# Two instead of four plain slices in the last feed-forward's first part, with the work around them in another order

## The chip, the cores and the metric

The kernel runs on one core of a Trainium2 chip. The metric is the device time of one execution in microseconds (us). TensorE (PE) does the matmuls and transposes, VectorE (DVE) and ScalarE (ACT) the elementwise work, SyncE's queue (SP) issues most transfers. Each engine works through its own instructions in a fixed order.

## The reference

One inference step of a decoder with two layers, in float32, for a prompt of 1024 tokens and 8 sample tokens that share all weights. Each layer has a mixer and a feed-forward, each between two RMS norms, with a residual behind. The part that the change is about is the feed-forward of the last layer:

```python
def swiglu(h, w_gu, w_down):
    gate, up = jnp.split(h @ w_gu, 2, axis=-1)
    return (jax.nn.silu(gate) * up) @ w_down

h = h + rmsnorm(mix, g[1])
h = h + rmsnorm(swiglu(rmsnorm(h, g[2]), w_gu[l], w_down[l]), g[3])
```

The model width is 1024, the hidden width of the feed-forward 2816, which is 22 slices of 128.

## The kernel before

**Two groups.** The tokens go through as two groups: group 0 holds 512 prompt tokens, group 1 the other 512 and the 8 sample tokens (520 columns, in two halves of 260). Activations lie transposed: 128 features on the partitions, tokens along the free dimension, eight tiles for the model width. Every float32 operand is split into two parts of a faster matmul type: ACT casts it (`split_to`, L286; `split_w`, L266), DVE subtracts the cast from the original, and three matmuls (high times high, high times low, low times high) stand for one.

**A feed-forward of group 1 in the last layer** is the class `ffn_w`. Its 22 slices come in five parts (`PARTS`: 5, 5, 4, 4, 4 slices); each part computes its slices and then projects them down (L696), added up in `R`. A slice is computed in one of two ways:

- *plain* (`gate_up_q`, L528): gate and up each as 8 blocks by 3 by 2 halves, together 96 matmuls of 260 columns and four weight blocks of 128 x 512;
- *seven products* (`gate_up_w`, L553): a scheme of the Strassen kind over 2 x 2 blocks of weights and tokens. Seven products of 12 matmuls (84), seven weight blocks (four of them sums that were put into DRAM earlier), and a few additions in PSUM and on DVE. Between products ACT puts negated partial results into other PSUM banks (L588, L591), DVE combines at the end (L599 to L605).

The products need sums of the token operands. `sums_w` (L355) makes them in four steps, each with 12 DVE rows of 260 columns (L369 full operand, L377 difference, L288 split) and four ACT casts. In part 0 the first four slices are plain (`plain` = 4), and between them the steps of `sums_w` are issued: one behind the first slice, two behind the second, one behind the third, each kept on DVE behind that slice's product of gate and up.

**What runs beside it.** Group 0's feed-forward of the same layer has just ended. Its closing (`f0.finish(False)`: row-sum matmul L332, Ln and Exp on ACT in L333 and L334, then `residual`, DVE rows L457 and L463), the transposes and stores of its output (`store_y`, L1555 to L1560) and the transposes of group 1's own residual into rows (`token_rows`, L513 to L524, which also frees the four buffers of `apool` that hold it) are woven between the steps of `ffn_w`: 17 of theirs to 7 of its. `weave` sets the order in which instructions are recorded; a scheduler then sets the order on each engine, and buffers are handed out from pools of fixed size (PSUM banks `q`, raw weights `w`, split weights `ws`). `residual` reads its input into buffers of the pool whose tag is `x0`, which `sums_w` uses too. From part 1 on, every other raw weight block lies in half a buffer of `apool` (`raws`).

Of the kernel before, what the change touches and what calls it, by code (L numbers as in the profile page):

```python
# [18 lines left out]
P = 128  # L19
# [5 lines left out]
def tile_decoder(  # L25
# [46 lines left out]
    def nm(s):  # L72
        uid[0] += 1
        return f"{s}_{uid[0]}"
# [159 lines left out]
    def weave(*streams):  # L234
        drain(mixed(*streams))
# [49 lines left out]

    def split_to(dst, src):  # L286
        nc.scalar.copy(dst[0], src)  # L287
        nc.vector.tensor_sub(dst[1], src, dst[0].bitcast(F32))  # L288

    def rev(ap):  # L290
        st, n = ap.ap[-1]
# [53 lines left out]
    def normed(g, R, rstd, gc, out, keep=False):  # L345
        n = NG[g]
        for k in range(ND):
            t = N() if keep else R[k]
            nc.vector.scalar_tensor_tensor(t[:, :n], R[k][:, :n], gc(k), rstd[:, :n], op0=ALU.mult, op1=ALU.mult)
            x = X(g)  # L350
            split_to((x[:, 0, :n], x[:, 1, :n]), t[:, :n])
            out.append(x)
            yield

    def sums_w(xs, ops):  # L355

        n, h = NG[1], PW[1]
        for k in range(4):  # L360
            x0, x1 = xs[k], xs[k + 4]
            y = YT()
            if k % 2 == 0:
                z, u = YT(), YT()
            o = (k % 2) * h

            def full(x, c):
                t = B()
                nc.vector.tensor_add(t[:, :h], x[:, 0, c : c + h].bitcast(F32), x[:, 1, c : c + h].bitcast(F32))  # L369
                return t  # L370

            b11, b12, b21, b22 = full(x0, 0), full(x0, h), full(x1, 0), full(x1, h)
            for d, p, a, b in (
                (b11, u[:, :, o : o + h], b12, b11), (b12, y[:, :, h : 2 * h], b12, b22),
                (b22, y[:, :, :h], b22, b11), (b21, z[:, :, o : o + h], b21, b22),
            ):
                nc.vector.tensor_sub(d[:, :h], a[:, :h], b[:, :h])  # L377
                split_to((p[:, 0, :], p[:, 1, :]), d[:, :h])
            ops.append([
                x0[:, :, :h], x1[:, :, :h], x1[:, :, h:n], z[:, :, o : o + h], u[:, :, o : o + h],  # L380
                y[:, :, :h], y[:, :, h : 2 * h],
            ])
            yield
# [54 lines left out]
            out.append(x)  # L438
            yield

    def residual(g, R, rstd, gc, store, acc=None, first=False):
        n = NG[g]
        w = D // 2 if first else n
        ht = [xpool.tile([P, 2, w], F32, tag=f"x{g}", name=nm("ht")) for _ in range(ND // 2)]
        for j in range(ND // 2):
            if first:
                t0 = g * G + j * P
                nc.sync.dma_start(ht[j].rearrange("p a n -> p (a n)"), x_prompt[0, t0 : t0 + P, :])
            else:
                nc.sync.dma_start(ht[j], hs[g][:, 2 * j : 2 * j + 2, :n])  # L450
        for k in range(ND):
            if first:
                ps = NS()
# [3 lines left out]
            nc.vector.scalar_tensor_tensor(R[k][:, :n], R[k][:, :n], gc(k), rstd[:, :n], op0=ALU.mult, op1=ALU.mult)  # L457
            if first:
                nc.vector.tensor_add(R[k][:, :G], R[k][:, :G], ps)
                if g:  # L460
                    nc.vector.tensor_add(R[k][:, G:n], R[k][:, G:n], xsraw[:, k, :])
            else:
                nc.vector.tensor_add(R[k][:, :n], R[k][:, :n], ht[k // 2][:, k % 2, :])  # L463
# [64 lines left out]
    def gate_up_q(l, f, xt):  # L528

        h, n = PW[1], NG[1]  # L530
        sg = T()
        for j in range(2):
            w = split_w(w_gu[l], 0, ND, j * DFF + f * P)
            pp = [Q(2 * j + a) for a in range(2)]
            for k in range(ND):
                wh, wl = w[k]
                for wi, (wt, xi) in enumerate(((wh, 0), (wh, 1), (wl, 0))):
                    for a in range(2):
                        nc.tensor.matmul(  # L539
                            pp[a][:, :h], wt, xt[k][:, xi, a * h : (a + 1) * h],  # L540
                            start=(k == 0 and wi == 0), stop=(k == ND - 1 and wi == 2),
                        )
            for a in range(2):
                d = sg[:, a * h : (a + 1) * h]
                if j == 0:
                    nc.scalar.activation(d, pp[a][:, :h], AF.Silu)
                else:
                    last = nc.vector.tensor_mul(d, d, pp[a][:, :h])
        mt = M(F32R)
        split_to((mt[:, 0, :n], mt[:, 1, :n]), sg[:, :n])  # L550
        return mt, last

    def gate_up_w(l, f, ops, spl, raws):  # L553

# [52 lines left out]
        split_to((mt[:, 0, :n], mt[:, 1, :n]), sg[:, :n])  # L607
        return mt

    sums = {}  # L610

    def part_of(f):
        for i, (f0, nf) in enumerate(PARTS):
# [30 lines left out]
    class ffn_w:  # L644


        def __init__(self, l, x, plain):
            self.g, self.l, self.x, self.ops, self.plain, self.n, self.r, self.pi = 1, l, x, [], plain, 0, 0, 0
            self.R = self.acc = None
            self.half = []  # L650
            self.sums = sums_w(x, self.ops)

        def spl(self):
            self.n += 1
# [13 lines left out]
        def part(self, pi):  # L668
# [4 lines left out]
            for j in range(nf):  # L673
                self.pi = pi
                if f0 + j < self.plain:
                    mt, ins = gate_up_q(l, f0 + j, self.x)
                    mids.append(mt)
                    with tc.issue_after(ins.ins):
                        for _ in range((1, 2, 1, 0)[j]):
                            next(self.sums, None)  # L680
                else:
                    mids.append(gate_up_w(l, f0 + j, self.ops, self.spl, self.raws))
                yield
# [33 lines left out]
    class ffn:  # L717
# [37 lines left out]
        def finish(self, store):  # L755
            rstd = rstd_from(self.acc, NG[self.g], 1.0 / D)
            acc = small([P, WID], tag="st", bufs=3) if store else None
            yield from residual(self.g, self.R, rstd, lambda k: gcol(self.l, 3, k), store, acc)
            if store:
                self.r = rstd_from(acc, NG[self.g], 1.0 / D)  # L760
                yield
# [863 lines left out]
    weave((o1.finish(), 17), (f0.part(4), 8))  # L1625
    banks.close()
    single.append(ctx.enter_context(tc.tile_pool(name="quads", bufs=2, space=PSUM)))
    f1 = ffn_w(1, o1.x, 4)
    weave((chain(f0.finish(False), store_y(0, f0.R), token_rows(1, o1.R)), 17), (chain(f1.part(0), f1.part(1)), 7))
    drain(f1.part(2), f1.part(3), f1.part(4), f1.finish_rows())  # L1630


# [30 lines left out]
```

## Time and profile before

| | us |
|---|---|
| median of 3 runs | 2450.96 |
| lowest and highest run | 2450.86, 2453.5 |
| the profiled execution | 2454.44 |
| its span, first to last instruction | 2452.7 |
| PE busy | 2413.9 |
| DVE busy | 1563.8 |
| ACT busy | 1204.3 |

The profiled execution is one more run of its own, and times in the trace count from the start of its span. A row of a timeline has start, duration, engine, line, operation, output and inputs by the program's names, and in brackets how long the engine stood idle before it and what ended that. Durations of neighbours overlap, so what an instruction costs its queue is the step from one start to the next. In the trace part 0 of the last feed-forward runs from 2070 to 2164 us.

### The profile page before, as it was taken

The page shows a single profiled execution, that of the slowest core. Times are in us where ns is not written, and L with a number is a line of the kernel's source. Part 1 is how long each engine was busy: PE and PEld are TensorE (multiplying, and loading weights), DVE is VectorE, ACT ScalarE, POOL GpSimd, SP SyncE. Part 2 cuts the span into 40 slices and gives each one's busy share as a digit, 9 for nine tenths or more (in the row PEclk, how much of TensorE's full clock was granted, in tenths as well). Part 3 has the DMA queues.
Part 4 walks back from the last instruction along what each step waited for, and adds up shares of the span by engine and source line. Part 5 has one row for each costly group of instructions (what it writes and reads, how often), then busy time and mean ns, then how long its engine had stood idle before and what let it go on. Part 6 is the DMA issues. An engine that isn't in the chain of part 4 may idle for free.

```text
span 2452.7 us, 40619 instructions
## 1 busy us (share of the span) xinstructions
PE 2413.9 (98%) x15473; PEld 2141.9 (87%) x15473; DVE 1563.8 (64%) x2697; ACT 1204.3 (49%) x2354; POOL 102.6 (4%) x153
## 2 busy tenths in 40 slices
PE   7999999999999999999999999999999999999998
PEld 5888988888877887999999989877787898999997
DVE  5777556765775676555544585677677558655665
ACT  4547544444444454555433454555454445564444
POOL 2000000000000000011111100022000000000000
PEclk9999999999999999999999999999999999999998
DMA  5353252263543446686688866453453244375541
GB/s 177 106 157 104 74 159 84 65 178 118 179 136 95 138 146 210 171 221 150 181 201 220 237 187 189 153 163 118 140 154 117 82 126 125 117 200 148 151 134 66
DMA packets 496726, 360.33 MB, mean 147 GB/s; under 512 B 19181, under 2 KB 443738, under 8 KB 496530
## 3 DMA queue, kind: packets, MB, share of 16 engines
q1 hardware_dynamic: 477970, 303.19, 41.2%
q0 software_dynamic: 18560, 54.53, 9.1%
q8 instruction: 122, 2.00, 0.3%
q14 instruction: 74, 0.61, 0.1%
HBM read 327.83 MB, written 75.96 MB: 165 GB/s over the span
## 4 chain that ended last, share of the span: by engine, by line
PE 90%; DVE 4%; DMA 2%; ACT 2%; issue 1%; SPq 0%; POOL 0%; DVEq 0%; ACTq 0%; POOLq 0%
PE mm L280 62%; PE q L581 7%; PE q L696 5%; PE q L539 2%; PE mm L1082 2%; PE s L932 1%; PE s L891 1%; PE s L1265 1%; PE mm L868 1%; PE s L1440 1%; PE mm L841 1%; DMA b<-qd 1%; PE s L1479 1%; PE s L918 1%; DVE ws L267 1%
## 5 line engine op out<-in xcount | busy, mean ns | idle before, releaser
L280 PE MATMUL mm<-x,ws 128*128 128x260 f32 (+1 forms) x7776 | 1330.4, 330 | 0.0
L280 PEld LDWEIGHTS mm<-x,ws 128*128 128x128 f32 x7776 | 1149.2, 188 | 142.9 <-issue 8.2
L266 ACT CAST ws<-w 128x512 fp32r<-128x512 f32 x712 | 420.1, 591 | 685.7 <-PE mm L280 563.6
L267 DVE TENSOR_TENSOR ws<-w,ws 128x512 fp32r<-128x512 f32 x712 | 462.1, 652 | 263.3 <-ACT ws L266 255.7
L280 PE MATMUL mm<-m,ws 128*128 128x512 f32 (+1 forms) x2112 | 393.1, 343 | 0.4 <-DVE r L476 0.4
L280 PEld LDWEIGHTS mm<-m,ws 128*128 128x128 f32 x2112 | 324.3, 189 | 47.3 <-issue 3.4
L696 PE MATMUL q<-m,ws 128*128 128x260 f32 x1056 | 128.8, 283 | 0.0
L696 PEld LDWEIGHTS q<-m,ws 128*128 128x128 f32 x1056 | 127.2, 188 | 0.4 <-ACT hT L514 0.2
L572 DVE TENSOR_TENSOR ws<-w,ws 128x512 fp32r<-128x512 f32 x126 | 86.5, 691 | 59.7 <-ACT ws L571 57.0
L581 PE MATMUL q<-y,ws 128*128 128x260 f32 x864 | 112.9, 283 | 0.0
L571 ACT CAST ws<-w 128x512 fp32r<-128x512 f32 x126 | 78.0, 621 | 67.9 <-PE q L696 27.4
L581 PEld LDWEIGHTS q<-y,ws 128*128 128x128 f32 x864 | 107.6, 188 | 0.0
L476 DVE TENSOR_TENSOR r<-r,mm 128x512 f32<-128x512 f32 (+1 forms) x96 | 66.0, 687 | 59.9 <-PE mm L280 58.8
L320 DVE TENSOR_SCALAR t<-mm 128x512 f32<-128x512 f32 (+1 forms) x74 | 51.2, 692 | 64.3 <-PE mm L280 64.3
L732 DVE TENSOR_TENSOR t<-t,mm 128x512 f32<-128x512 f32 (+1 forms) x66 | 45.5, 689 | 67.9 <-PE mm L280 67.4
L324 DVE TENSOR_TENSOR t<-t,t 128x512 f32<-128x512 f32 (+1 forms) x66 | 45.8, 694 | 65.7 <-ACT t L323 65.7
L581 PE MATMUL q<-x,ws 128*128 128x260 f32 x648 | 86.3, 282 | 0.0
L581 PEld LDWEIGHTS q<-x,ws 128*128 128x128 f32 x648 | 81.3, 188 | 0.0
L343 DVE TENSOR_TENSOR st<-st,n 128x512 f32<-128x512 f32 (+1 forms) x98 | 67.1, 691 | 6.5 <-ACT n L342 5.0
L287 ACT CAST m<-t 128x512 fp32r<-128x512 f32 (+1 forms) x88 | 54.9, 624 | 25.3 <-DVE t L732 16.5
L1018 POOL DMA_INDIRECT c<-in_cache_sb_k,pidx x16 | 16.4, 1026 | 1128.7 <-issue 919.7
L288 DVE TENSOR_TENSOR m<-t,m 128x512 fp32r<-128x512 f32 (+1 forms) x88 | 60.9, 692 | 2.6 <-ACT m L287 1.4
(356 smaller groups left out, 2513.0 us busy)
## 6 DMA issues: line engine op xcount, KB each, us to landing
w<-in_w_gu SPq DMA_DIRECT2D x334, 256.0 KB, 3.1
w<-in_w_down SPq DMA_DIRECT2D x160, 256.0 KB, 2.7
w<-in_w_in_a SPq DMA_DIRECT2D x80, 256.0 KB, 2.9
wsum<-in_w_gu POOLq DMA_DIRECT2D x18, 1024.0 KB, 8.9
w<-wsum SPq DMA_DIRECT2D x72, 256.0 KB, 3.5
w<-in_w_o SPq DMA_DIRECT2D x64, 256.0 KB, 2.7
wsum<-in_w_gu POOLq DMA_DIRECT2D x12, 1280.0 KB, 10.5
w<-in_w_mem_kv SPq DMA_DIRECT2D x32, 256.0 KB, 3.2
```

Source lines behind the costliest of these rows:

```text
L266: nc.scalar.copy(ws[:, 0, :n, :], raw[:, :n, :])
L267: nc.vector.tensor_sub(ws[:, 1, :n, :], raw[:, :n, :], ws[:, 0, :n, :].bitcast(F32))
L280: nc.tensor.matmul(ps[:, a, : PW[g]], wt, xt[k][:, xi, o : o + PW[g]], start=(k == 0 and wi == 0), stop=(k == nk - 1 and wi == 2),)
L287: nc.scalar.copy(dst[0], src)
L288: nc.vector.tensor_sub(dst[1], src, dst[0].bitcast(F32))
L320: nc.vector.tensor_scalar(sv(x, g), pv(ps, g), -44.0, None, op0=ALU.max)
L343: nc.vector.tensor_add(acc[:, :n], acc[:, :n], t[:, :n])
L476: nc.vector.tensor_add(dst, dst, pv(ps, g))
L571: nc.scalar.copy(w[:, 0, :], src)
L572: nc.vector.tensor_sub(w[:, 1, :], src, w[:, 0, :].bitcast(F32))
L581: nc.tensor.matmul(ps[:, :h], w[:, wj, k * P : (k + 1) * P], x[:, xi, :], start=(first and k == 0 and wi == 0), stop=(k == 3 and wi == 2), ...
L696: nc.tensor.matmul(pp[a][:, :h], wt, mids[k][:, xi, a * h : (a + 1) * h], start=(k == 0 and wi == 0), stop=(k == nf - 1 and wi == 2),)
```

## The change

It does four things in the last part. Two slices instead of four are plain, so that 192 matmuls become 168. All four steps of `sums_w` are issued behind the last split of the norm ahead of them (`done`), two after each plain slice, instead of behind the slices' own products. The closing residual of group 0 reads its input into the pool `cpool` (`spare`). And the weave is taken apart: two plain slices alone, then the closing residual and the store of group 0 between the three product slices, then the token rows between the steps of part 0's down projection, then part 1.

```diff
     def split_to(dst, src):
         nc.scalar.copy(dst[0], src)
-        nc.vector.tensor_sub(dst[1], src, dst[0].bitcast(F32))
+        return nc.vector.tensor_sub(dst[1], src, dst[0].bitcast(F32))
...
-            split_to((x[:, 0, :n], x[:, 1, :n]), t[:, :n])
+            ins = split_to((x[:, 0, :n], x[:, 1, :n]), t[:, :n])
             out.append(x)
+            if k == ND - 1:
+                done.append(ins)
...
-        ht = [xpool.tile([P, 2, w], F32, tag=f"x{g}", name=nm("ht")) for _ in range(ND // 2)]
+        ht = [C() if spare else xpool.tile([P, 2, w], F32, tag=f"x{g}", name=nm("ht")) for _ in range(ND // 2)]
...
             self.sums = sums_w(x, self.ops)
+            self.after = done[-1]
...
                 if f0 + j < self.plain:
-                    mt, ins = gate_up_q(l, f0 + j, self.x)
-                    mids.append(mt)
-                    with tc.issue_after(ins.ins):
-                        for _ in range((1, 2, 1, 0)[j]):
-                            next(self.sums, None)
+                    mids.append(gate_up_q(l, f0 + j, self.x))
+                    with tc.issue_after(self.after.ins):
+                        next(self.sums, None)
+                        next(self.sums, None)
...
-    f1 = ffn_w(1, o1.x, 4)
-    weave((chain(f0.finish(False), store_y(0, f0.R), token_rows(1, o1.R)), 17), (chain(f1.part(0), f1.part(1)), 7))
+    f1 = ffn_w(1, o1.x, 2)
+    first = f1.part(0)
+    drain(islice(first, 2))
+    weave((chain(f0.finish(False), store_y(0, f0.R)), 12), (islice(first, 3), 3))
+    weave((token_rows(1, o1.R), 5), (first, 4))
+    drain(f1.part(1))
     drain(f1.part(2), f1.part(3), f1.part(4), f1.finish_rows())
```

Where this moves instructions is shown at three places. Lines stand two further down in the changed kernel from here on (L457 is L459, L546 is L548, L571 is L573). DVE, right behind the last split of the norm (`x`), before; `r` is group 0's sum, `ht` its residual input, `ws` split weights:

```order
L288 TENSOR_TENSOR x_20237<-n_20235,x_20237 128x520
L288 TENSOR_TENSOR x_20242<-n_20240,x_20242 128x520
L457 SCALAR_TENSOR_TENSOR r_16324<-r_16324,par,st_20030 128x512 x2
L463 TENSOR_TENSOR r_16324<-r_16324,ht_20255 128x512 x2
L457 SCALAR_TENSOR_TENSOR r_16324<-r_16324,par,st_20030 128x512
L267 TENSOR_TENSOR ws_20428<-w_20426,ws_20428 128x512
```

After the change the same two rows are followed by 56 others (all the sums and the two plain slices' own rows); these are the last two of them and what stands behind:

```order
L288 TENSOR_TENSOR y_20574<-b_20581,y_20574 128x260
L288 TENSOR_TENSOR y_20552<-b_20579,y_20552 128x260
L574 TENSOR_TENSOR ws_20615<-w_20613,ws_20615 128x512
L574 TENSOR_TENSOR ws_20633<-w_20631,ws_20633 128x512
L574 TENSOR_TENSOR ws_20650<-w_20648,ws_20650 128x512
L574 TENSOR_TENSOR ws_20668<-w_20666,ws_20668 128x512
L288 TENSOR_TENSOR m_20548<-t_20423,m_20548 128x520
L459 SCALAR_TENSOR_TENSOR r_16324<-r_16324,par,st_20030 128x512
L574 TENSOR_TENSOR ws_20687<-w_20685,ws_20687 128x512
L465 TENSOR_TENSOR r_16324<-r_16324,c_20599 128x512
```

The sums (`y`) now stand ahead of the first weight split of a product slice (L574) and the closing residual behind it, between that slice's splits.

ACT, around the closing's Ln (L333) and Exp (L334), before:

```order
L333 ACTIVATE st_20030<-q_20251,epsb 128x512
L287 CAST x_20242<-n_20240 128x520
L334 ACTIVATE st_20030<-st_20030 128x512
L266 CAST ws_20428<-w_20426 128x512
L546 ACT_TABLE_LOAD
L546 ACTIVATE t_20265<-q_20276 128x260
```

And after the change, where L590 is the product slice's first negation and L596 its Silu:

```order
L333 ACT_TABLE_LOAD
L333 ACTIVATE st_20030<-q_20595,epsb 128x512
L287 CAST m_20548<-t_20423 128x520
L334 ACT_TABLE_LOAD
L334 ACTIVATE st_20030<-st_20030 128x512
L590 ACTIVATE q_20610<-q_20609 128x260
L573 CAST ws_20708<-w_20706 128x512
L573 CAST ws_20726<-w_20724 128x512
L593 ACTIVATE q_20611<-q_20610 128x260
L573 CAST ws_20761<-w_20759 128x512
L596 ACT_TABLE_LOAD
L596 ACTIVATE t_20683<-q_20609 128x260
```

Ln and Exp have moved from ahead of the first plain slice's Silu (L546) into the first product slice, and three more table loads stand there.

PE, at the end of the token rows (the sample rows, `8x128`, out of the `apool` buffers `a`), before, where part 0's down projection follows:

```order
L523 MATMUL q_21303<-ident,a_19138 8x128 x2
L523 MATMUL q_21303<-ident,a_19139 8x128 x2
L523 MATMUL q_21309<-ident,a_19140 8x128 x2
L523 MATMUL q_21309<-ident,a_19141 8x128 x2
L696 MATMUL q_21325<-m_20390,ws_21317 128x260
```

And after the change, where part 1's first product follows:

```order
L525 MATMUL q_21499<-ident,a_19138 8x128 x2
L525 MATMUL q_21499<-ident,a_19139 8x128 x2
L525 MATMUL q_21505<-ident,a_19140 8x128 x2
L525 MATMUL q_21505<-ident,a_19141 8x128 x2
L583 MATMUL q_21511<-x_20075,ws_21517 128x260 x3
```

The sample rows' transposes have moved from ahead of 120 of the down projection's matmuls to behind all of them. On ACT their two copies (`c`) now stand directly ahead of part 1's first weight casts:

```order
L705 COPY r_21106<-q_21465 128x260
L526 COPY c_21498<-q_21499 8x512
L526 COPY c_21498<-q_21505 8x512
L573 CAST ws_21517<-w_21515 128x512
L573 CAST ws_21535<-w_21533 128x512
L573 CAST ws_21552<-w_21550 128x512
```

Of these blocks `w_21533` is the first that lies in half an `apool` buffer.

More of the change, by code (lines that the diff above doesn't have):

```diff
@@ L439, in start, with residual @@
             yield
-    def residual(g, R, rstd, gc, store, acc=None, first=False):
+    def residual(g, R, rstd, gc, store, acc=None, first=False, spare=False):
         n = NG[g]
         w = D // 2 if first else n
-        ht = [xpool.tile([P, 2, w], F32, tag=f"x{g}", name=nm("ht")) for _ in range(ND // 2)]
+        ht = [C() if spare else xpool.tile([P, 2, w], F32, tag=f"x{g}", name=nm("ht")) for _ in range(ND // 2)]
         for j in range(ND // 2):
@@ L547, in gate_up_q @@
                 else:
-                    last = nc.vector.tensor_mul(d, d, pp[a][:, :h])
+                    nc.vector.tensor_mul(d, d, pp[a][:, :h])
         mt = M(F32R)
         split_to((mt[:, 0, :n], mt[:, 1, :n]), sg[:, :n])
-        return mt, last
+        return mt
     def gate_up_w(l, f, ops, spl, raws):
@@ L608, in gate_up_w @@
         return mt
-    sums = {}
+    sums, done = {}, []
     def part_of(f):
@@ L757, in finish @@
             acc = small([P, WID], tag="st", bufs=3) if store else None
-            yield from residual(self.g, self.R, rstd, lambda k: gcol(self.l, 3, k), store, acc)
+            yield from residual(self.g, self.R, rstd, lambda k: gcol(self.l, 3, k), store, acc, spare=not store)
             if store:
```

## The prediction

> **What bounds the kernel now.** I read the page's busy shares first, then the table of stretches near the change, then the timelines of TensorE (PE), VectorE (DVE), ScalarE (ACT) and the DMA queue SP in the stretch that the change rewrites.
>
> ```profile
> PE 2413.9 (98%) x15473; PEld 2141.9 (87%) x15473; DVE 1563.8 (64%) x2697; ACT 1204.3 (49%) x2354; POOL 102.6 (4%) x153
> ```
>
> ```profile
> core 0: us, PE busy (x) PEld busy (x) DVE busy (x) ACT busy (x) POOL busy (x), PEclk, DMA share, GB/s
> 2050.00:2100.00 50.00, 48.25 (x323) 43.89 (x322) 48.45 (x90) 26.90 (x48) 0.00 (x0) 1.00 0.28 82
> 2100.00:2150.00 50.00, 50.00 (x424) 49.56 (x423) 28.30 (x63) 28.10 (x65) 0.00 (x0) 1.00 0.41 130
> ```
>
> PE is busy through all of it and the clock is granted in full, so a matmul taken out is worth its own time, and every wait that is put before a matmul costs its own time. The other number to see is DVE between 2050 and 2100: 48.45 of 50 us. DVE is as full as PE just where the change hangs more work in front of PE.
>
> ```profile
> 2070.47 2.03 PE L539 MATMUL q<-x,ws 128*128 128x260 f32 x15 [1.75 <-DVE r L476]
> 2072.33 1.02 PE L332 MATMUL q<-st,ones 128*128 128x512 f32 x2
> 2072.79 44.70 PE L539 MATMUL q<-x,ws 128*128 128x260 f32 x369
> 2117.33 1.91 PE L1555 MATMUL q<-ident,r 128*128 128x128 f32 x16
> ...
> 2127.72 1.61 PE L581 MATMUL q<-y,ws 128*128 128x260 f32 x12
> 2129.16 1.91 PE L1555 MATMUL q<-ident,r 128*128 128x128 f32 x16
> ...
> 2148.90 1.04 PE L523 MATMUL q<-ident,a 128*8 128x128 f32 x8
> 2149.82 14.60 PE L696 MATMUL q<-m,ws 128*128 128x260 f32 x120
> 2164.26 1.59 PE L581 MATMUL q<-x,ws 128*128 128x260 f32 x12
> ```
>
> Lines of the changed kernel stand two further down than these, so L581 is L583 there. These rows are the four plain slices (L539), one slice of seven products (L581), the down projection of part 0 (L696) and the start of part 1 (2164.26). No row after the first has a bracket: PE waits for nothing from 2070.47 to 2164.26.
>
> **Term 1, matmuls saved: -3.0 us.** The 369 plain matmuls begin every (2117.33 - 2072.79) / 369 = 0.1207 us, so a plain slice of 96 takes 11.6 us; a product of 12 takes 1.44 us (2127.72 to 2129.16), a slice of seven 10.1. Two slices change kind: 2 x 1.5 = 3.0 us less. Transposes and down projection stay the same in number. A product slice loads, casts and splits seven weight blocks where a plain one has four: six more loads on SP, casts on ACT and splits on DVE. The loads lie beside (DMA is 0.28 to 0.41 busy above), the splits are counted in term 2.
>
> **Term 2, the first product slice waits for DVE: +4.3 us (2.5 to 6).** DVE works in order. What an instruction takes from the next one there is read from these rows:
>
> ```profile
> 2075.25 1.41 DVE L457 SCALAR_TENSOR_TENSOR r<-r,par,st 128x512 f32<-128x512 f32 x2
> 2076.57 1.28 DVE L463 TENSOR_TENSOR r<-r,ht 128x512 f32<-128x512 f32 x2
> ...
> 2085.74 0.42 DVE L369 TENSOR_TENSOR b<-x 128x260 f32<-128x260 f32 x1
> 2086.08 0.42 DVE L377 TENSOR_TENSOR b<-b,b 128x260 f32<-128x260 f32 x1
> 2086.42 0.68 DVE L463 TENSOR_TENSOR r<-r,ht 128x512 f32<-128x512 f32 x1
> 2087.02 0.42 DVE L288 TENSOR_TENSOR y<-b,y 128x260 fp32r<-128x260 f32 x1
> ```
>
> A 260-wide row takes 0.34 us of the queue (2085.74 to 2086.08), a 512-wide one 0.60 (2086.42 to 2087.02), a scale-and-multiply of 512 takes 0.66 (1.32 for two). The last norm row leaves DVE at 2075.25, and nothing ahead of it changes on DVE. Before, the closing residual of the first half stands there. Now the 56 rows up to the first weight split of a product slice are 48 rows of operand sums (16.3), 4 products with up (1.4), one middle split and three weight splits (2.4): 20.1 us, so that split starts at 2095.4 and is ready 0.7 later, at 2096.1. ACT's casts for the sums are as many as before and lie beside.
>
> PE gets there earlier: 2070.47 + 192 x 0.1207 = 2093.6, and 0.46 for the row-sum matmul L332 (2072.33 to 2072.79, moved here) makes 2094.1. Four matmuls need only the cast half of their weights (0.5), then PE waits from 2094.6 to 2096.1: 1.5 us.
>
> Next on DVE, up to the first split of the third and last product slice: 14 weight splits and 2 middle splits (9.6), the closing residual's eight L457-kind rows (5.3) and eight L463-kind rows (4.8), six rows of the slices' combinations (2.0) = 21.7, so that slice's weights are ready at 2117.8. PE wants them after 14 products (20.2) and 8 transposes (1.91 / 16 x 8 = 0.9): at 2115.2. So the wait is 2.5 us in all even if DVE never waits itself. But it does, in two ways. Behind the first product slice's last product, DVE has a combination row (L606 after the change), a residual row and only then the next slice's weight split: 0.2 (a product's last matmul ends that long after the next has begun: 1.61 against 1.44) + 0.34 + 0.66 + 0.68 = 1.9 us, against which PE has four transposes and two matmuls (0.7), so 1.2 more. And the residual's root-mean-square chain is now issued in the middle of the product slice, where it costs ACT table loads:
>
> ```profile
> 2073.39 0.69 ACT L333 ACTIVATE st<-q,epsb 128x512 f32<-128x512 f32 x1
> 2073.98 0.62 ACT L287 CAST x<-n 128x520 fp32r<-128x520 f32 x1
> 2074.50 0.63 ACT L334 ACTIVATE st<-st 128x512 f32<-128x512 f32 x1
> 2075.03 0.61 ACT L266 CAST ws<-w 128x512 fp32r<-128x512 f32 x1
> 2075.65 1.28 ACT L546 ACT_TABLE_LOAD   x1
> ...
> 2120.72 0.37 ACT L588 ACTIVATE q<-q 128x260 f32<-128x260 f32 x1 [0.54 <-PE q L581]
> ```
>
> Before, Ln (L333) and Exp (L334) ran with the table that was there and one load followed, Silu's. Now Silu's load comes first, then Ln, Exp and Silu again each bring one: three loads more, 3.8 us of ACT. Behind Exp's load waits ACT's negation of the first product (L590), which PE's third product adds onto. ACT is through it at 2094.6 + 1.3 (load) + 0.6 (Ln) + 0.5 (a middle cast) + 1.3 (load) + 0.5 (Exp) + 0.4 (the negation, L588 now) = 2099.2; PE's first two products end at 2096.1 + 20 x 0.12 = 2098.5. That is 0.7 more. 2.5 + 1.2 + 0.7 = 4.4; since these waits partly overlap DVE's own lateness, I take 4.3. The lower end is DVE's sum alone, 2.5; the upper end adds two further handovers of 0.8 us each (one for each remaining slice).
>
> The closing residual's input now has buffers of its own and is read long ahead; no wait for it is seen now, so this is worth nothing here. The store's and the rows' transposes now come eight banks in a row, 3.7 us of PE; ACT's and DVE's evictions at some 0.6 each run beside them on two engines, so I cost them at nothing (if one engine had to do all eight alone, 1.1).
>
> **Term 3, part 1 starts late: +3.0 us (2.0 to 4.7).** Now the sample rows' transposes (L523) come at 2148.90, 15.4 us before part 1. After the change they are the last thing ahead of part 1. They free the buffers into which the second weight block of part 1 is loaded:
>
> ```profile
> SPq L566 <- PE q L523: 1.0, 1, 1.0
> ```
> ```profile
> 2149.31 1.08 SPq L566 DMA_DIRECT2D w<-wsum  x2
> ```
> ```profile
> 2150.12 1.05 ACT L524 COPY c<-q 8x512 f32<-8x512 f32 x2
> 2152.84 0.62 ACT L571 CAST ws<-w 128x512 fp32r<-128x512 f32 x1 [1.67 <-DMA w<-wsum]
> ...
> 2153.58 0.65 ACT L703 COPY r<-q 128x260 f32<-128x260 f32 x2
> ```
> ```profile
> L566 SPq DMA_DIRECT2D w<-wsum x17: 359/377/775, 2149.3 to 2178.8; - x17
> DMA to landing us min/median/max: 3.5/4.1/5.5
> ```
>
> SP waited for L523, issued the block 0.41 us after its start, and ACT's cast waited for the landing until 2152.84: 3.94 us from L523's start. Hidden now under 120 matmuls of 14.4 us; after the change nothing hides it. Let F be the start of these eight transposes after the change. They end at F + 0.92 (2148.90 to 2149.82). ACT evicts part 0's last sums (L703, from 0.1 to 0.75), makes the two sample copies (1.05, to 1.8) and casts the first block (to 2.4), DVE splits it (to 3.15), and PE ends product 1 at F + 4.4. The second block is cast from 3.95 to 4.55, split to 5.25, and product 2 ends at 5.25 + 10 x 0.12 = 6.5. Unhindered it would end at 0.92 + 2.88 = 3.8: 2.7 us lost, 3.3 with the median landing of 4.1. I take 3.0. ACT's order alone, with the block there in time, gives 2.0; the slowest landing, 5.5, gives 4.7.
>
> **Sum.** -3.0 + 4.3 + 3.0 = +4.3 us; from the terms' bounds +1.5 to +7.7. The profiled execution took 2454.44 us (span 2452.7, 1.7 around it), so it would take 2458.7. It is 3.5 us above the median of the runs, 2450.96; that median becomes 2455.3. Seen along PE, part 1's transposes end some 1.3 us later than now, and its second product 4.3. Behind them PE's order is the same to the end; PE is full there, so nothing is given back.
>
> **A rule of the skill.** These rows at the end of the kernel show a switch of tables between two functions:
>
> ```profile
> 2441.33 0.24 ACT L788 ACTIVATE rr<-q,epsb 8x1 f32<-8x1 f32 x1
> 2441.58 1.28 ACT L786 ACT_TABLE_LOAD   x1
> 2442.88 0.20 ACT L786 ACTIVATE rr<-rr 128x4 f32<-128x4 f32 x1
> ```
>
> The load begins as the function before it ends (2441.57) and the next function starts 0.02 us behind it. So I price a load at 1.3. The Trainium skill, "ScalarE: Activation LUTs", section "What ACT_TABLE_LOAD costs", says that every switch also drains the engine for about 1.38 us, some 2.66 in all; by that the two loads ahead of L590 would cost 2.8 us more, and the sum would be +7.1. This case's trace does not agree: there is no such gap.
>
> **The rivals.**
> - *Slower by more than 0.2%: the loads for part 1.* Price and place are term 3's. 0.2% (4.9 us) is about what a measurement of this kernel can tell from no change. With term 2 as worked out, the sum passes 4.9 once term 3 passes 3.6, which is a landing 4.4 us after issue. For it: half of 17 such loads took 4.1 or more, up to 5.5, and SP issues all of part 1's loads in a burst there. Against: the one that matters took 3.5. At 5.5 the sum is -3.0 + 4.3 + 4.7 = +6.0, 2457.0 us.
> - *The table loads hold ACT longer than 1.3.* A load that waited for ACT to run empty would hold L590 and the first residual row, which needs Exp. At twice the seen 1.3 for each of the two: +2.6, sum +6.9, 2457.9 us. Against: the three rows above. The Trainium skill's rule named above would be this case.
> - *The cover holds.* PE waits only the 1.5 us at the first product slice, and part 1's start is hidden: -3.0 + 1.5 = -1.5, 2449.5; with no wait at all -3.0, 2448.0. It needs DVE to do 41.8 us of rows in less time than they take now, and part 1's blocks to be in other buffers than those that the sample rows free. The page's 64% for DVE speaks for it, the 48.45 of 50 us in the stretch itself against it.
>
> **How the numbers follow.** The forecast (both waits appear, +1.5 to +6): 0.60, of which a quarter lies above 4.9. The loads: 0.20. The table loads: 0.05. The cover holds: 0.15, a third of it by something that I do not see and that gains over 4.9. Slower by over 0.2%: 0.15 + 0.20 + 0.05 = 0.40; faster: 0.05; within 0.2%: 0.55. The range goes from the cover's 2449.5 to 2459.5, which is 0.8 above the bounds' +7.7, for the spread of the runs before (2450.86 to 2453.5).
>
> **What would show it.** In the changed kernel's profile: PE's first L583 rows show a wait for DVE's weight split L574 of about 1.5 us near 2094.6, and another of about 1.2 before the second product slice; ACT shows three table loads between 2094 and 2104; PE's row after the sample transposes L525 waits for ACT and DVE, and ACT there for the DMA from the summed weights. If PE has no bracket at L583, term 2 is wrong; if part 1's first two products run without one, term 3 is. If the first product slice starts later than 2094.2, something ahead of it moved that I held fixed. A time under 2449 would mean that a wait outside this stretch went.

## The result and the profile after

| | before | changed |
|---|---|---|
| median of 12 runs each, us | 2451.64 | 2457.15 |
| lowest and highest, us | 2450.86, 2454.59 | 2455.61, 2461.25 |
| profiled execution, us | 2454.44 | 2458.15 |
| its span, us | 2452.7 | 2456.4 |

The changed kernel is slower: ratio 1.0021, 95% interval 1.0014 to 1.0029, that is 3.4 to 7.1 us, 5.1 in the middle; the medians differ by 5.5. The two executions whose traces are compared differ by 3.7.

The page's busy times first, then the two stretches that the prediction read:

```profile
PE 2413.9 (98%) x15449; PEld 2140.0 (87%) x15449; DVE 1568.2 (64%) x2707; ACT 1213.2 (49%) x2369; POOL 104.1 (4%) x153
```

```profile
core 0: us, PE busy (x) PEld busy (x) DVE busy (x) ACT busy (x) POOL busy (x), PEclk, DMA share, GB/s
2050.00:2100.00 50.00, 46.57 (x305) 41.69 (x304) 47.66 (x102) 33.10 (x61) 0.00 (x0) 1.00 0.26 75
2100.00:2150.00 50.00, 48.41 (x405) 47.96 (x405) 33.01 (x62) 29.55 (x66) 0.00 (x0) 1.00 0.53 164
```

24 matmuls are gone, but PE's busy time is what it was. In the stage that is compared below it is only 0.8 us less (97.31 after 98.11), since a row that waits part-way reads longer (the two matmuls at 2093.38 take 0.81 us, the two at 2094.44 take 0.48), and the rest of the execution happens to have 0.8 more. PE is no longer full in the stretch: 46.57 and 48.41 of 50 us, where it had 48.25 and 50.00. The clock is granted in full. PE's timeline shows where:

```profile
2069.89 23.20 PE L541 MATMUL q<-x,ws 128*128 128x260 f32 x192 [1.75 <-DVE r L478]
...
2093.38 0.81 PE L583 MATMUL q<-x,ws 128*128 128x260 f32 x2
2094.44 0.48 PE L583 MATMUL q<-y,ws 128*128 128x260 f32 x2 [0.26 <-DVE t L550]
2095.63 1.46 PE L583 MATMUL q<-x,ws 128*128 128x260 f32 x10 [0.71 <-DVE ws L574]
2096.93 1.36 PE L583 MATMUL q<-y,ws 128*128 128x260 f32 x10
2099.01 1.71 PE L583 MATMUL q<-y,ws 128*128 128x260 f32 x12 [0.71 <-ACT q L590]
...
2106.82 0.60 PE L1557 MATMUL q<-ident,r 128*128 128x128 f32 x4
2108.68 1.47 PE L583 MATMUL q<-x,ws 128*128 128x260 f32 x10 [1.27 <-DVE ws L574]
...
2110.61 2.91 PE L583 MATMUL q<-y,ws 128*128 128x260 f32 x22 [0.33 <-ACT q L590]
...
2129.61 2.78 PE L1557 MATMUL q<-ident,r 128*128 128x128 f32 x24
...
2164.44 1.03 PE L525 MATMUL q<-ident,a 128*8 128x128 f32 x8
2166.70 0.51 PE L583 MATMUL q<-x,ws 128*128 128x260 f32 x2 [1.22 <-ACT ws L573]
...
2172.14 1.60 PE L583 MATMUL q<-x,ws 128*128 128x260 f32 x12
```

Brackets stand in four places where there was none: the start of the first product slice (for DVE's splits), its third product (for ACT's L590), the second product slice, and the start of part 1. What a place costs is read from the starts, since the brackets leave out what a started matmul waits.

**One number for the stage.** Executions also differ ahead of 2065 us (the last section shows why), so I compare a stage: from the first plain matmul (or the first transposes beside it) to part 1's fourth product. Ahead of it and behind it every kernel of this document has the same number of matmuls (12397 and 2260), and behind it each takes 283.9 to 284.5 us more. Before: 2070.47 to 2168.58, 98.11 us. Changed: 2069.89 to 2172.14, 102.25 us, so **+4.14**. In part 0 the three product slices with eight transposes would take 21 x 1.444 + 8 x 0.115 = 31.2 us; they took 2129.61 - 2093.38 = 36.2, so **5.0** are waits. The sample transposes should have handed over to part 1 at 2164.44 + 0.92, and the fourth product should have begun three products (4.33) later, at 2169.7; it began at 2172.14: **2.45**. Against these stand the saved matmuls, -2.8 (a plain slice 192 / 2 matmuls in 11.52, a slice of products 10.11), and some -0.5 for transposes and plain matmuls, which ran a little closer.

### The profile page after: what moved, and what is told of

Same layout as the page of the kernel before. It is cut to its first block, busy times and chain, and to the rows that moved or that the text cites. A ratio compares the mean times of both kernels' runs of the same rounds, so it can differ in the third digit from the quotient of the medians.

```text
span 2456.4 us, 40607 instructions
## 1 busy us (share of the span) xinstructions
PE 2413.9 (98%) x15449; PEld 2140.0 (87%) x15449; DVE 1568.2 (64%) x2707; ACT 1213.2 (49%) x2369; POOL 104.1 (4%) x153
## 4 chain that ended last, share of the span: by engine, by line
PE 90%; DVE 5%; ACT 2%; DMA 2%; issue 1%; SPq 0%; POOL 0%; DVEq 0%; ACTq 0%; POOLq 0%
PE mm L280 63%; PE q L583 8%; PE q L698 5%; PE mm L1084 2%; PE s L934 1%; PE s L893 1%; PE s L1267 1%; PE s L1442 1%; PE mm L843 1%; PE mm L870 1%; PE s L1481 1%; DMA b<-qd 1%; PE s L920 1%; PE s L1469 1%; DVE ws L267 1%
## 5 line engine op out<-in xcount | busy, mean ns | idle before, releaser
L574 DVE TENSOR_TENSOR ws<-w,ws 128x512 fp32r<-128x512 f32 x140 | 94.9, 690 | 57.7 <-ACT ws L573 54.8
L583 PE MATMUL q<-y,ws 128*128 128x260 f32 x960 | 126.4, 284 | 1.5 <-ACT q L590 1.0
L583 PEld LDWEIGHTS q<-y,ws 128*128 128x128 f32 x960 | 119.6, 188 | 2.3 <-ACT q L590 1.4
L573 ACT CAST ws<-w 128x512 fp32r<-128x512 f32 x140 | 86.0, 620 | 67.2 <-PE q L698 27.0
L583 PE MATMUL q<-x,ws 128*128 128x260 f32 x720 | 97.1, 283 | 3.4 <-DVE ws L574 2.2
L583 PEld LDWEIGHTS q<-x,ws 128*128 128x128 f32 x720 | 90.5, 188 | 4.9 <-DVE ws L574 2.9
```

What stands on the lines that cost most here:

```text
L573: nc.scalar.copy(w[:, 0, :], src)
L574: nc.vector.tensor_sub(w[:, 1, :], src, w[:, 0, :].bitcast(F32))
L583: nc.tensor.matmul(ps[:, :h], w[:, wj, k * P : (k + 1) * P], x[:, xi, :], start=(first and k == 0 and wi == 0), stop=(k == 3 and wi == 2), ...
```

## The experiments

Each ran against the kernel before on the same chip. E1 to E4, E5 with E9 to E11, and E12 shared their runs of it (medians 2452.9, 2452.1 and 2452.28 us). E5 has 5 runs, the other experiments 11. No runs stand under the numbers E6 to E8. The stage is read from the PE timeline of each kernel's one profiled execution.

| kernel | median us | ratio to before (95%) | stage us | stage less before |
|---|---|---|---|---|
| changed | 2457.15 | 1.0021 (1.0014 to 1.0029) | 102.25 | +4.14 |
| E1 rows earlier | 2455.37 | 1.0011 (1.0002 to 1.0020) | 100.51 | +2.40 |
| E2 Ln and Exp earlier | 2457.47 | 1.0017 (1.0008 to 1.0026) | 103.53 | +5.42 |
| E3 four plain slices | 2454.09 | 1.0005 (0.9996 to 1.0014) | 99.58 | +1.47 |
| E4 rows between plain slices | 2455.68 | 1.0013 (1.0004 to 1.0022) | 100.97 | +2.86 |
| E5 two plain slices alone | 2459.62 | 1.0036 (1.0022 to 1.0050) | 105.76 | +7.65 |
| E9 three plain, E1, E2 | 2455.16 | 1.0010 (1.0001 to 1.0019) | 101.97 | +3.86 |
| E10 E4 and E2 | 2450.89 | 0.9995 (0.9986 to 1.0004) | 96.40 | -1.71 |
| E11 fewer sums | 2454.38 | 1.0012 (1.0003 to 1.0021) | 101.33 | +3.22 |
| E12 E10, residual spread | 2450.38 | 0.9993 (0.9984 to 1.0002) | 97.08 | -1.03 |

Stage and time go together: each median's difference from that of before is within 1.4 us of the stage's, so to that accuracy what happens to the time happens between 2065 and 2175 us.

**E1, the token rows twice as dense, so that they end within the down projection.**

```diff
-    weave((token_rows(1, o1.R), 5), (first, 4))
+    weave((token_rows(1, o1.R), 10), (first, 4))
```

> The changed kernel with the token rows woven twice as fast into part 0's down projection, so that the sample rows' transposes and the freeing of the buffers come 120 matmuls before part 1; nothing ahead of the down projection moves. Theory (two separate waits, one in front of the product slices for DVE and ACT, about 5.0 us, one at part 1's start for the late buffers and ACT's copies, about 2.5 us; matmuls saved about 3 us): the wait at part 1 goes and the one in part 0 stays, so 2.5 us faster than the changed kernel, 2.0 to 3.0 us slower than before (ratio 1.001). Rival (the loss is one thing, DVE's lateness, and part 1's wait is only its tail): no change from the changed kernel, 5 us slower than before (1.002).

PE of E1 around the start of part 1:

```profile
2147.27 1.04 PE L525 MATMUL q<-ident,a 128*8 128x128 f32 x8
2148.18 14.60 PE L698 MATMUL q<-m,ws 128*128 128x260 f32 x120
2162.62 1.59 PE L583 MATMUL q<-x,ws 128*128 128x260 f32 x12
...
2166.95 1.60 PE L583 MATMUL q<-x,ws 128*128 128x260 f32 x12
```

As expected: the sample transposes L525 stand 120 matmuls ahead of part 1 again and its brackets are gone. The stage is 1.74 shorter than the changed kernel's (part 1's wait was 2.45); part 0's waits stay, and come to 5.5 in this execution. The two waits are separate, and the second is made by where L525 stands.

**E2, the closing's row-sum, Ln and Exp ahead of part 0.**

```diff
-    first = f1.part(0)
+    first, fin = f1.part(0), f0.finish(False)
+    next(fin)
     drain(islice(first, 2))
-    weave((chain(f0.finish(False), store_y(0, f0.R)), 12), (islice(first, 3), 3))
+    weave((chain(fin, store_y(0, f0.R)), 11), (islice(first, 3), 3))
```

> The changed kernel with the closing's row sums, Ln and Exp and its first residual row ahead of the plain slices again, so that the three added table loads are gone; the other seven residual rows and all sums stay. Theory: the waits behind ACT's negations (0.9 and 0.5 us) go; the first wait for a weight split grows by the 1.3 us of the one residual row that is now ahead of it, and the later ones shrink by as much; together 1 to 2 us faster than the changed kernel, 3 to 4 us slower than before, and the wait at part 1's start stays at 2.5. Rival (the table loads are the main cost, each with a drain as the skill says): the loss in part 0 goes nearly altogether, 4 us or more faster than the changed kernel, about 1 us slower than before.

A miss: no gain. The table loads went, but so did what held the residual back. In a count of DVE's rows from the first plain matmul to the first split of a product slice, E2 has two residual pairs and a middle split that the changed kernel has behind that split. Of that count the group of the first kind of residual row (L465 has two as well), and then the split in E2's DVE timeline:

```profile
L459 DVE SCALAR_TENSOR_TENSOR r<-r,par,st 128x512 f32<-128x512 f32 x2 | 1.5, 742 | 0.0
```
```profile
2095.89 3.09 DVE L574 TENSOR_TENSOR ws<-w,ws 128x512 fp32r<-128x512 f32 x5
```

2 x (0.66 + 0.60) + 0.6 = 3.1 us more ahead of the split, which comes 27.98 us behind the first plain matmul (2095.89 - 2067.91) where the changed kernel has 25.00 (2094.89 - 2069.89). PE waited 4.2 us, and its 10 and 22 matmuls behind that, up to the next row quoted, were slow:

```profile
2096.63 2.11 PE L583 MATMUL q<-x,ws 128*128 128x260 f32 x10 [4.19 <-DVE ws L574]
...
2102.08 1.60 PE L583 MATMUL q<-x,ws 128*128 128x260 f32 x12
```

The 32 matmuls took 2102.08 - 2096.63 = 5.45 us where 0.12 each make 3.85: 1.6 lost to a lower clock (last section). Behind them part 0 has no bracket: the waits for ACT's negations are gone with the loads, and what they cost came back as one wait for DVE. Since the edit moved residual rows together with the loads, it doesn't price the loads alone; it shows that nothing is won while DVE is the later of the two.

**E3, the changed kernel with four plain slices.**

```diff
-    f1 = ffn_w(1, o1.x, 2)
+    f1 = ffn_w(1, o1.x, 4)
```

> The changed kernel with four plain slices: the new order alone, without the saved matmuls. Theory: DVE has two plain slices more (23 us of PE) before the first product slice, so all waits in part 0 go; the matmuls are back; part 1's wait of 2.5 us stays as the only loss: 2 to 3 us slower than before (1.001). Rival (the new order as such costs time in part 0, not the missing cover): 5 us or more slower than before (1.002 and above).

The direction held, the size was smaller (+1.47 in the stage): part 0 has no wait but one of 0.18, and part 1's shrank to some 1.2. PE and then ACT of E3 there:

```profile
2162.48 1.68 PE L583 MATMUL q<-x,ws 128*128 128x260 f32 x12
2164.69 3.61 PE L583 MATMUL q<-y,ws 128*128 128x260 f32 x24 [0.52 <-ACT q L590]
```
```profile
2162.33 1.05 ACT L526 COPY c<-q 8x512 f32<-8x512 f32 x2
2164.26 0.37 ACT L590 ACTIVATE q<-q 128x260 f32<-128x260 f32 x1 [0.88 <-PE q L583]
```

No cast stands between the sample copies (L526) and the first negation: the first products had their weights cast earlier. So in the new order it is the lack of the two plain slices that brings part 0 its waits; the price of the late rows depends on what ACT has cast ahead.

**E4, the token rows between the two plain slices.**

```diff
-    drain(islice(first, 2))
+    weave((token_rows(1, o1.R), 5), (islice(first, 2), 2))
     weave((chain(f0.finish(False), store_y(0, f0.R)), 12), (islice(first, 3), 3))
-    weave((token_rows(1, o1.R), 5), (first, 4))
+    drain(first)
```

> The changed kernel with the token rows between the two plain slices instead of in the down projection: part 1's buffers are free 60 us ahead, and PE has 4.2 us of transposes more to do before the first product slice, while DVE has no more to do there (the rows' copies are ACT's). Theory: part 1's wait goes (2.5 us), and PE reaches the first product slice 4.2 us later, so the first wait for DVE (1.8 us) goes too; DVE's own floor behind it shrinks by as much; in all 4 to 5 us faster than the changed kernel, within 1 us of before. Rival (ACT, which gets ten copies more beside the sums' casts, holds the sums back): the wait before the first product slice stays at 1.5 us or more and the kernel is 2 us or more slower than before.

A miss by some 2 us. Part 1's wait went, and the first product slice started without one, since PE's transposes gave DVE time. But DVE, which was on time, then stood still:

```profile
2100.83 0.75 DVE L459 SCALAR_TENSOR_TENSOR r<-r,par,st 128x512 f32<-128x512 f32 x1 [4.46 <-ACT st L334]
2101.50 0.68 DVE L574 TENSOR_TENSOR ws<-w,ws 128x512 fp32r<-128x512 f32 x1
```
```profile
2096.60 1.28 ACT L333 ACT_TABLE_LOAD   x1
...
2098.88 1.28 ACT L334 ACT_TABLE_LOAD   x1
2100.17 0.63 ACT L334 ACTIVATE st<-st 128x512 f32<-128x512 f32 x1
```

The first residual row needs Exp, and Exp comes behind two loads; the next weight split stands behind that row on DVE, and its cast behind Exp on ACT. DVE never caught up: PE waited 1.00 us for a combination row (L601), 0.91 for the second slice's split and 1.26 for that slice's L601, and part 0's waits came to 5.5. So Ln and Exp with their loads are a second price, hidden in the changed kernel by the late sums, where DVE waited 0.72 for the same Exp.

**E5, the kernel before with two plain slices and nothing else.**

```diff
-                        for _ in range((1, 2, 1, 0)[j]):
+                        for _ in range((2, 2)[j]):
...
-    f1 = ffn_w(1, o1.x, 4)
+    f1 = ffn_w(1, o1.x, 2)
```

> The kernel before with two plain slices instead of four and two steps of sums behind each: the saved matmuls alone, in the old order. Theory: 3 us of matmuls go; DVE has to do the closing residual and all sums (some 42 us of rows with the splits) before the last product slice can start, as in the changed kernel, so 3 to 5 us of waits come in part 0; the sample rows stay 120 matmuls ahead of part 1, so no wait there. Together 0 to 2 us slower than before. Rival (the loss comes from the new order, not from the two plain slices): 3 us faster than before (0.9988).

Slower than either theory gave. One row of E5's PE, and a group of its DVE rows from the first plain matmul to the first seven-product slice's third split (lines as before the change):

```profile
2099.36 2.54 PE L581 MATMUL q<-y,ws 128*128 128x260 f32 x10 [2.66 <-ACT y L287]
```
```profile
L457 DVE SCALAR_TENSOR_TENSOR r<-r,par,st 128x512 f32<-128x512 f32 x6 | 4.3, 747 | 0.0
```

Here PE waits for the operand sums themselves (`y`): six residual rows of the L457 kind stand ahead of or between them on DVE. Two plain slices give too little cover for sums and residual together; the change's other parts (sums first, residual behind) won back about 3.5 of these 7.65 us, of which some 1.7 were a lower clock behind the wait shown (last section).

**E9, three plain slices with E1's rows and E2's Exp.**

```diff
-    f1 = ffn_w(1, o1.x, 2)
-    first = f1.part(0)
+    f1 = ffn_w(1, o1.x, 3)
+    first, fin = f1.part(0), f0.finish(False)
+    next(fin)
...
-    weave((token_rows(1, o1.R), 5), (first, 4))
+    weave((token_rows(1, o1.R), 10), (first, 4))
```

> The changed kernel with three plain slices, token rows woven twice as fast and the closing's row sums, Ln and Exp ahead of the plain slices. Theory: one slice's 1.5 us of matmuls are saved, DVE has 11.5 us more before the first product slice so that the first wait goes, no table loads are added, no wait at part 1: 0.5 to 1.5 us faster than before. Rival (waits for DVE remain whenever sums and closing are ahead of product slices): 1 us or more slower than before.

A miss. E2's order came back: the third plain slice waited for its split behind sums and residual rows, and the clock fell again (PE):

```profile
2100.35 12.31 PE L541 MATMUL q<-x,ws 128*128 128x260 f32 x88 [3.03 <-DVE ws L267]
2112.50 1.36 PE L583 MATMUL q<-x,ws 128*128 128x260 f32 x10
```

88 matmuls took 12.15 us instead of 10.6.

**E10, E4's rows with E2's Exp.**

```diff
-    first = f1.part(0)
-    drain(islice(first, 2))
-    weave((chain(f0.finish(False), store_y(0, f0.R)), 12), (islice(first, 3), 3))
-    weave((token_rows(1, o1.R), 5), (first, 4))
+    first, fin = f1.part(0), f0.finish(False)
+    next(fin)
+    weave((token_rows(1, o1.R), 5), (islice(first, 2), 2))
+    weave((chain(fin, store_y(0, f0.R)), 11), (islice(first, 3), 3))
+    drain(first)
```

> The changed kernel with the token rows between its two plain slices and the closing's row sums, Ln and Exp ahead of them. In the run with the token rows there alone, DVE stood 4.5 us at the first residual row, waiting for Exp, with the weight splits behind it. Theory: with Exp done early that stand goes, PE's 4.2 us of transposes cover the sums, the added table loads and part 1's wait are gone: 1 to 2.5 us faster than before. Rival (DVE's sum of rows bounds the stage in any order): waits of 3 us or more remain in part 0 and the kernel is no faster than before.

PE of E10: the first product slice starts without a bracket, one wait is left, and the last row ends the stage, which began at 2066.55:

```profile
2095.10 1.68 PE L583 MATMUL q<-x,ws 128*128 128x260 f32 x12
...
2104.66 1.73 PE L583 MATMUL q<-y,ws 128*128 128x260 f32 x12 [0.67 <-DVE t L601]
...
2162.95 1.60 PE L583 MATMUL q<-x,ws 128*128 128x260 f32 x12
```

Part 0's waits are 1.0 (2095.10 to 2127.32 less 31.2), part 1's none, and the saved 2.8 show: -1.71. Either edit alone left waits of 5.5 (E4) and 5.9 (E2, 1.6 of it by the clock) in part 0; together they leave 1.0. E4's lets PE arrive later, by its transposes, and E2's keeps Exp out of DVE's way. The time is 1.2 us under before with an interval that includes no change, and well under the changed kernel's.

**E11, the changed kernel with 16 rows of sums left out.** L371's additions are dropped, the sums taken from the cast halves (the lines left out give the differences buffers of their own).

```diff
-                t = B()
-                nc.vector.tensor_add(t[:, :h], x[:, 0, c : c + h].bitcast(F32), x[:, 1, c : c + h].bitcast(F32))
-                return t
+                return x[:, 0, c : c + h].bitcast(F32)
...
```

> The changed kernel with the 16 DVE additions left out that put the operands' high and low parts together for the sums: the sums are made of the high parts alone, so the output is less exact. DVE has 5.4 us less to do ahead of the first product slice. Theory: the first wait (1.8 us) goes; the first residual row still waits for Exp, which comes at the same time as before, so the waits behind it stay (about 3 us), and part 1's 2.5 us stay: 1.5 to 2.5 us faster than the changed kernel, about 3 us slower than before. Rival (DVE's sum of rows alone sets all waits in part 0): they all go, 4.5 to 5 us faster than the changed kernel, within 0.5 us of before.

The theory's side against the rival: the kernel stays slower than before, by 2.3 us by the medians and 3.2 in the stage, where some 3 were expected. Against the changed kernel the gain was less than expected: 16 x 0.34 = 5.4 us of DVE less bought only 0.9 in the stage instead of 1.5 to 2.5. The first wait shrank from 1.8 to 0.4, and DVE stood instead (lines one lower here):

```profile
2097.40 0.75 DVE L458 SCALAR_TENSOR_TENSOR r<-r,par,st 128x512 f32<-128x512 f32 x1 [3.52 <-ACT st L334]
```

**E12, E10 with the residual woven 8 to 3.**

```diff
-    weave((chain(fin, store_y(0, f0.R)), 11), (islice(first, 3), 3))
+    weave((chain(fin, store_y(0, f0.R)), 8), (islice(first, 3), 3))
```

> As the kernel with token rows between the two plain slices and the closing's Ln and Exp ahead of part 0, but the closing residual and the store are woven 8 to 3 into the product slices instead of 11 to 3, so that DVE has fewer residual rows between a slice's weight splits. Theory (part 0's waits are DVE's order: a residual row pair ahead of a split or a combination delays PE): the one wait left there, 0.67 us before a product for the combination row L601, goes, the stage comes out at about 95.5 us against 98.11 before the change, and the time is 1.5 to 2.5 us less than before the change. Rival (what is left is the floor of DVE's sum, and the rows that move back pile up ahead of the third product slice or of the down projection): within 0.5 us of the 11 to 3 kernel, 0.7 to 1.7 us less than before the change.

The wait that was to go, for L601, is still there:

```profile
2105.49 1.72 PE L583 MATMUL q<-y,ws 128*128 128x260 f32 x12 [0.78 <-DVE t L601]
```

The stage is 0.7 longer than E10's, and the time, 1.9 us under before by its median and 0.5 under E10's, can't be told from it. The theory was not put to the test at this place: in both kernels two residual pairs and a split stand on DVE between the split at 2100.45 (2101.27 in E12) and L601. Nor does the rival's floor, DVE's sum of rows, show, since DVE stood still ahead of that split. E10's DVE:

```profile
2100.45 0.69 DVE L574 TENSOR_TENSOR ws<-w,ws 128x512 fp32r<-128x512 f32 x1 [0.87 <-ACT ws L573]
```

ACT's cast for this split had waited 2.01 us for its weight block to land (2.31 in E12, where DVE then stood 1.18), and from the split to L601 DVE has no gap. So the chain to the last wait goes through that late block and the residual pairs behind it; no run takes away one of them alone. E10 and E12 beat the changed kernel; that they beat the one before is likely, but neither interval shows it.

## Why the prediction was right, point by point

The median predicted was 2455.3; 2457.15 was measured, within the range. The sum was +4.3; the stage gave +4.14, the profiled executions +3.7, the medians +5.5. Of the 1.85 between the two medians, 0.7 is the kernel before, whose median rose from 2450.96 in 3 runs to 2451.64 in 12. By its chances the forecast held a time within 0.2% of before (0.55) for likelier than a slower one (0.40); 0.21% was measured, with an interval on both sides of 0.2%. Both waits came where they were forecast. That the sum meets the stage to 0.2 us is in part luck: the terms below are off by +0.2, +0.7 and -0.55, and some -0.5 for plain matmuls and transposes that ran closer was in no term.

- **Term 1**, -3.0: -2.8. The slices are as priced.
- **Term 2**, +4.3: 5.0, right in mechanism and 0.7 short in size. The first wait was to be 1.5: four matmuls of 0.5 took from 2093.38 to 2095.63, so 1.8, in two pieces; the first, for L550's product with up, was not seen ahead. The negation was to cost 0.7: ten matmuls of 1.2 from 2096.93 to 2099.01, 0.9. The handover was to cost 1.2: 1.4 (four transposes of 0.46 from 2106.82 to 2108.68). A further 0.5 ahead of 2110.61, where L590 comes late once more, was not in the sum. The 2.5 that DVE's total was to set by the third slice did not bind apart from these: behind 2110.61 there is no bracket in part 0. So 1.0 of the sum, the part of those 2.5 beyond the first wait, did not come about as described, and other waits filled its place. DVE was close behind, though: its first split for the third slice started at 2118.22, and PE reached that slice at 2119.38.
- **ACT's chain** went as laid out, three table loads in all. ACT of the changed kernel:

```profile
2093.82 0.41 ACT L287 CAST y<-b 128x260 fp32r<-128x260 f32 x1
2094.24 1.28 ACT L333 ACT_TABLE_LOAD   x1
2095.53 0.69 ACT L333 ACTIVATE st<-q,epsb 128x512 f32<-128x512 f32 x1
...
2096.76 1.28 ACT L334 ACT_TABLE_LOAD   x1
2098.05 0.63 ACT L334 ACTIVATE st<-st 128x512 f32<-128x512 f32 x1
2098.59 0.37 ACT L590 ACTIVATE q<-q 128x260 f32<-128x260 f32 x1
...
2101.82 1.28 ACT L596 ACT_TABLE_LOAD   x1
```

  Each load begins as the row ahead of it ends and the function follows 0.01 us behind it. The rival that loads hold ACT longer is refuted for these three. The Trainium skill's drain of 1.38 us per switch ("ScalarE: Activation LUTs", section "What ACT_TABLE_LOAD costs") is not in these rows either.
- **Term 3**, +3.0: 2.45. DVE's and ACT's order was as written, and the second block's landing came 3.55 us behind L525's start instead of 3.94:

```profile
2166.03 0.61 ACT L573 CAST ws<-w 128x512 fp32r<-128x512 f32 x1
2167.99 1.66 ACT L573 CAST ws<-w 128x512 fp32r<-128x512 f32 x3 [1.35 <-DMA w<-wsum]
```

  Some 1.8 of the 2.45 were lost by the end of part 1's first product (due at 2166.80, ended at about 2168.6), by ACT's order alone; the late block added the rest. The rival of the loads, decided by a landing over 4.4, did not occur: the time is past 0.2% by other terms. E1 takes this term away alone.
- **The cover holds**: refuted here (both waits are there), but E10 shows what it asked for: work for PE ahead of the product slice while DVE catches up, and Exp and the rows elsewhere.
- **Costed at nothing**: none of the eight L465 rows waits for the closing's own buffers (`c`). The lump of 24 transposes is followed by the next group after 2.6 us, 24 x 0.11, so the evictions did lie beside.

Where my reading was short is the experiments' misses: I took DVE's rows, Ln and Exp, and the rows of the store as terms to be added or taken away one by one. In E2, E4 and E11 the one that was left set the end.

## What to carry to other kernels

An engine's queue hands a late input on to all that stands behind it: in E4 DVE stood 4.46 us at one row that needed Exp, with the weight splits behind it. So before a piece is moved out of the way, list what will then be last at the same place, and move them together; E2 and E4 each left part 0 as long as it was or longer, and both together took 4 us of waits from it. In these runs, transposes and other work without weights were worth most where DVE had to catch up (E10), and least ahead of a part whose loads they release (E1).

## What was not expected of the hardware

The clock that PE was granted fell to one half behind some waits, and it was not the length of the wait alone that decided it. In the traces the low clock lasts 3.41 us each time, but for the end of the kernel. E2 around its gap of 4.19 us (the granted clock is the number behind POOL's count), the stretch ahead of the low one and the low one:

```profile
2093.74:2097.15 3.41, 0.52 (x4) 0.52 (x5) 3.41 (x8) 0.41 (x1) 0.00 (x0) 1.00 0.00 0
2097.15:2100.56 3.41, 3.41 (x18) 3.41 (x18) 3.26 (x7) 0.99 (x2) 0.00 (x0) 0.50 0.74 212
```

Half rate for 3.41 us is 1.7 us of missing clock, and the matmuls lost 1.6. E9's low stretch starts at 2101.01 and E5's at 2099.14; in the 3.41 us ahead of them PE was busy for 0.65 and 0.78.

Shorter waits did it too, and not every time. At one place long ahead of the change, PE waits 2.29 us in the changed kernel (until 1842.49) and 2.33 us in E2 (until 1842.09). First the changed kernel, then E2:

```profile
1839.66:1843.07 3.41, 1.12 (x8) 0.71 (x7) 3.41 (x5) 0.00 (x0) 0.00 (x0) 1.00 0.05 18
1843.07:1846.48 3.41, 3.41 (x10) 2.63 (x9) 3.41 (x6) 0.83 (x2) 0.00 (x0) 0.50 0.44 136
```
```profile
1837.74:1841.15 3.41, 2.02 (x11) 1.39 (x9) 3.34 (x3) 0.18 (x1) 0.00 (x0) 1.00 0.17 51
1841.15:1844.56 3.41, 2.48 (x13) 2.15 (x14) 3.41 (x6) 0.41 (x1) 0.00 (x0) 1.00 0.47 153
```

The wait lies within one stretch in the first and is divided between two in the second. The stretches lie on a grid that does not start with the wait: within each trace that has several, the starts of low clock are whole multiples of 3.413 us apart (945.37 and 1843.07 in the changed kernel, 263.0 of them; 1845.01 and 2101.01 in E9, 75.0). With all eleven traces cut along their grids, from 25 to 2430 us, PE was busy for 0.15 to 0.54 of each of the twelve stretches ahead of a low one, and for 0.45 or more of every other one at full clock (matmuls' ends are modelled, so these shares are rough). So in these kernels a wait cost up to 1.7 us more than itself where it left PE idle for about half of such a stretch or more, and where the stretches begin differed from one execution to the next.

Ahead of the stage, two low stretches lie in the traces of the kernel before, the changed one and E9, one in E3, E5 and E11, and none in E1, E2, E4, E10 and E12, though that part is the same in all: a reason to compare a stage. Within the stage E2, E5 and E9 have one each, up to 1.7 us of their difference; whether every execution of these three has it, no run shows. The Trainium skill, "TensorE: Matmul & The Clock Gate", section "What's actually happening", gives half rate after an idle window of about 3.4 us and full rate after a busy one, and calls the window free-running. Its length and its free run agree with these traces; but the windows ahead of half rate were not idle here, with PE busy for up to 0.54 of one.
